# Full array shapes for the products that use 64 rows, 16 rows, 64 columns or 16 columns

## The chip, the cores and the metric

The kernel runs on one core of a Trainium2 chip. The metric is device time in microseconds (us) of one execution; the runs shown are whole executions of the program. A core has five engines with instruction queues of their own: TensorE (PE; its weight loads are listed as PEld), VectorE (DVE), ScalarE (ACT), GpSimd (POOL) and SyncE (SP), which here issues nearly all DMAs.

## The reference

Two transformer blocks run one after the other on 2048 tokens of width 1024, all in float32. The first has eight heads of "forgetting" attention (causal, with a bias from cumulated gates) and eight query heads of sliding-window attention over two key heads, with a sink. The second puts 16 meta tokens in front of the sequence; its attention chooses 256 keys for each query by an index score and always sees the meta tokens, beside a gated linear recurrence (HGRN2):

```python
s = jnp.einsum('bnqhgd,bnshd->bnhgqs', qb, kk, ...) * (d ** -0.5)      # sliding window: 128 queries x 256 keys
...
s_h = jax.nn.relu(jnp.einsum('bqhd,bkd->bqhk', qib, ki_r)... * (IDX_DIM ** -0.5))
s_idx = jnp.einsum('bqhk,bqh->bqk', s_h, wib.astype(jnp.float32))      # index score, 4 heads of 64
s_idx = jnp.where(causal[None], s_idx, -jnp.inf)
_, sel = lax.top_k(s_idx, k_top)                                       # 256 keys of each query
...
p = jax.nn.softmax(jnp.concatenate([lg_m, lg_s], axis=-1), axis=-1)    # meta keys and chosen keys
return (jnp.einsum('bhqm,bmc->bqhc', p[..., :N_META], c_m) + jnp.einsum('bqhk,bqkc->bqhc', p[..., N_META:], c_sel))
...
new_state = (jnp.exp(b_last[:, :, 0, :])[..., None] * state            # HGRN2, chunks of 64
             + jnp.einsum('bhsk,bhsv->bhkv', kc * jnp.exp(b_last - bcum), vc))
```

## The kernel before

Float32 operands are split into a high and a low float16 half, and a product is done as high x high, high x low and low x high into one float32 accumulator. `load_q` and `load_k` put a head's queries and keys into tiles of 128 rows with two planes. Plane 0 (`QA`, `KA`) holds the high half in rows 0 to 63, and a few rows more below it for terms that are added by the product itself: rows 64 and 65 of `KA` hold two powers of two (from `d_kc`), and rows 64 and 65 of `QA` are written later, by `Att.max_rows`, with each query's row maximum cut into these two steps. Plane 1 (`QB`, `KB`) holds the cross terms of high and low in 128 rows.

A head goes through two passes. `prepare` loads it and computes scores in the orientation queries x keys from the high halves alone, to find each query's maximum on VectorE; `max_rows` then turns the maxima into rows 64 and 65 of `QA`. `main` computes the scores again as keys x queries with all terms (`QA` over 66 rows, then `QB`), lets `Att.weights` take the exponential (ScalarE), its float16 high half (ScalarE or VectorE) and the low half (GpSimd or VectorE), and multiplies the weights with the values in `Att.pv` by three products of 65, 64 and 65 columns. `weave` puts the steps of the next head's `prepare` between those of the current head's `main`, so that TensorE's queue mixes both; the steps are placed and ordered by a planner that works from a model of the engines' times. A head is prepared one or two heads ahead, and its tiles come from pools of two buffers, for which the loads wait in SyncE's queue.

The stages in order of time: prologue, projections and forgetting attention of heads 0 to 3 (to some 700 us); heads 4 to 7 with the sliding-window heads woven in, and the output projection (to 1420); index keys, queries and scores of the second block (`Index.scores`, to 1850), with latents between them; the second block's projections (to 2250); the second attention in four query groups g of 512 queries and eight heads each, with the recurrence's chunks and the output projection filled in (`phase_dsa`, to the end).

How the products stand that the change touches:

- The first attention's scores (L959) use 69 rows: 64 and five bias rows.
- The sliding-window scores (L852) and the second attention's scores (L2049) and meta scores (L2061) in `prepare` use rows 0 to 63 of `QA` and `KA`. On L2061 the four query tiles meet 16 meta keys each.
- `Index.scores` sets up queries `QI` in 128 rows (the high half twice) against keys `KI` (high half above low half), and a second product (L1472) of the low queries `QL` in 64 rows against the first 64 rows of `KI`.
- In `phase_dsa.main`, `meta` computes the 16 meta keys x 512 queries (L2083, L2084, and in the first query group L2087 for the bias), so 16 columns of the array are used; the weights of 16 rows then go through `pv` as products over 16 rows (L777 to L779).
- In `Hgrn.chunk` the last of seven scan levels (m = 64) uses 64 columns (L1917 to L1919), the others 128.

Of the kernel before, what the change touches and what calls it, by code (L numbers as in the profile page):

```python
# [10 lines left out]
F32 = mybir.dt.float32  # L11
# [710 lines left out]
class Att:  # L722
# [15 lines left out]

    def weights(self, s, ci):

        K = self.K
        nc = K.nc
        m, n = s.shape
        p = self.pp.tile([128, 512], F32, name="p32")[:m, :n]
        hi = self.pp.tile([128, 512], F16, name="phi")[:m, :n]
        lo = self.pp.tile([128, 512], F16, name="plo")[:m, :n]
        nc.scalar.activation(p, s, AF.Exp, scale=ci[:m], bias=K.shift[:m])  # L747
        if self.pick("hi", n):
            nc.scalar.copy(hi, p)  # L749
        else:  # L750
            nc.vector.tensor_copy(hi, p)
        e = nc.gpsimd if self.pick("lo", n) else nc.vector
        e.tensor_tensor(lo, p, hi, op=ALU.subtract)  # L753
        return hi, lo
# [49 lines left out]
class Swa:  # L804
# [31 lines left out]
    def prepare(self, g, h):  # L836
        K, op, sm = self.K, self.op, self.sm
        nc = K.nc
        if h % 4 == 0:
            self.load(g, h // 4)  # L840
        KA = self.keys[g, h // 4][0]
        Q = op.tile([128, 2, 512], F16, name="sQ")
        load_q(K, Q, K.d_qb, h, g * 512)
        QA, QB = Q[:, 0], Q[:, 1]
        mx = sm.tile([128, 4], F32, name="smx")
        es = sm.tile([128, 4, 1], F32, name="es")

        def score(s):
            k0 = 128 if g == 0 and s == 0 else s * 128
            w = 128 if g == 0 and s == 0 else 256  # L850
            p = self.ps1.tile([128, 512], F32, name="p1")
            nc.tensor.matmul(p[:, :w], lhsT=QA[:64, s * 128:s * 128 + 128], rhs=KA[:64, k0:k0 + w],  # L852
                             start=True, stop=True)
            jk = sm.tile([128, 256], BF, name="jk", bufs=1)
            nc.vector.tensor_tensor_reduce(jk[:, :w], p[:, :w], K.mR2[:, 256 - w:], 1.0, self.sks[:, h:h + 1],
                                           op0=ALU.add, op1=ALU.max, accum_out=mx[:, s:s + 1])

        def rows():
            z = self.at.max_rows(mx, QA)
            nc.vector.scalar_tensor_tensor(es[:, :, 0], z[:, :, 64], STEPS[0] / STEPS[1], z[:, :, 65], op0=ALU.mult,  # L860
                                           op1=ALU.add)
            nc.scalar.activation(es, es, AF.Exp, scale=self.ci[:, h // 4:h // 4 + 1], bias=self.sk[:, h:h + 1])

        return (QA, QB, es), [lambda s=s: score(s) for s in range(4)] + [rows]
# [377 lines left out]
def phase_proj2(K, A, E, finish):  # L1242
    nc, tc = K.nc, K.tc
    K.wbufs, K.rbufs, K.wpool = 6, 4, WPOOL[1]
    with ExitStack() as st:
# [47 lines left out]
        def latent(p, m, col, inv):  # L1293
# [32 lines left out]
            for t in range(tn):  # L1326
# [7 lines left out]
                if tw < 128:  # L1334
                    nc.gpsimd.memset(v2, 0.0)
                nc.gpsimd.memset(v2[:, :, 0:1], 1.0)
                split2(K, v2[:tw, :, 1:65], v2[:tw, :, 65:129], pv.rearrange("p (h d) -> p h d", h=8), 2.0 ** -20)
# [109 lines left out]
class Index:  # L1447
# [11 lines left out]
    def scores(self, i):  # L1459
        K, sc, KI, wi = self.K, self.sc, self.KI, self.wi  # L1460
        nc = K.nc
        QI = sc.tile([128, 4, 128], F16, name="QI")
        QL = sc.tile([64, 4, 128], F16, name="QL")
        for (dst, a) in ((QI[:64], 0), (QI[64:], 0), (QL, 1)):
            nc.sync.dma_start(dst, ap(K.d_qi, a * S + i * 128, [[2 * S, 64], [128 * S, 4], [1, 128]]))
        for u in range(i // 4 + 1):
            w = min(512, (i + 1) * 128 - u * 512)
            acc, ac2 = (sc.tile([128, 512], F32, name=n, bufs=b)[:, :w] for n, b in (("acc", 2), ("ac2", 1)))
            for h in range(4):
                p = self.psc.tile([128, 512], F32, name="psc")  # L1470
                nc.tensor.matmul(p[:, :w], lhsT=QI[:, h], rhs=KI[:, u * 512:u * 512 + w], start=True, stop=False)
                nc.tensor.matmul(p[:, :w], lhsT=QL[:, h], rhs=KI[:64, u * 512:u * 512 + w], start=False, stop=True)  # L1472
                t, f = (acc, ac2)[h % 2], wi[:, i, h:h + 1]
# [337 lines left out]
class Hgrn:  # L1811
# [58 lines left out]
    def chunk(self, t):  # L1870
# [35 lines left out]
        for li, m in enumerate(LEVELS):  # L1906
# [6 lines left out]
            p = self.py.tile([128, 8, 64], F32, name="pl", tag="y")  # L1913
            M = 64 if m == 64 else 128
            for h in range(8):
                qv = [x[:, h].rearrange("p (n a m) -> p n a m", a=2, m=m)[:, :, 1] for x in (hi, lo)]
                nc.tensor.matmul(p[:M, h], lhsT=hi[:, h, :M], rhs=qv[0], start=True, stop=False)  # L1917
                nc.tensor.matmul(p[:M, h], lhsT=hi[:, h, :M], rhs=qv[1], start=False, stop=False)
                nc.tensor.matmul(p[:M, h], lhsT=lo[:, h, :M], rhs=qv[0], start=False, stop=True)  # L1919
            if m == 64:  # L1920
# [58 lines left out]
def phase_dsa(K, A, out):  # L1979

    nc, tc = K.nc, K.tc
    with ExitStack() as st:
# [12 lines left out]

        jr, jb = K.jr, K.jb
        lg = os_.tile([128, D], F32, name="lg")
        lb = wp.tile([128, D], F32, name="lbb")
# [18 lines left out]
        def prepare(g, h, mk):  # L2017
            n = (g + 1) * 512
            x = "0" if g == 0 and h % 2 == 0 else ""
            Q = op.tile([128, 2, 512], F16, name="QA", tag="QA" + x)  # L2020
            load_q(K, Q, K.d_q2, h, g * 512)
            QA, QB = Q[:, 0], Q[:, 1]

# [12 lines left out]
            if g == 0:  # L2036

                bM = op.tile([16, 2, 256], F32R, name="bM")
                bMb = op.tile([16, 128], BF, name="bMb")
                nc.sync.dma_start(f32(bM), ap(K.d_rb, h * 512 + 128, [[1, 16], [8 * 512, 2], [1, 256]]))  # L2040
                nc.sync.dma_start(bMb, ap(K.d_rbb, h * 512 + 128, [[1, 16], [1, 128]]))
            mu = sm.tile([128, 4, 5], F32, name="mu", tag="mu" if g else "mu0")[:, :, :g + 2]

            def score(s, u):
# [3 lines left out]
                near = [(j, 0 if j == i else 128) for j in (i - 1, i) if j >= 0 and j // 4 == u]  # L2048
                nc.tensor.matmul(p[:, :w], lhsT=QA[:64, s * 128:s * 128 + 128], rhs=KA[:64, 16 + u * 512:16 + u * 512 + w],  # L2049
                                 start=True, stop=not near)  # L2050
# [7 lines left out]
            def meta():  # L2058
                p = ps1.tile([128, 512], F32, name="p1")
                for s in range(4):  # L2060
                    nc.tensor.matmul(p[:, s * 16:s * 16 + 16], lhsT=QA[:64, s * 128:s * 128 + 128],  # L2061
                                     rhs=KA[:64, :16], start=s == 0, stop=False, skip_group_check=True)
                if g == 0:
                    nc.tensor.matmul(p[:, :16], lhsT=bMb, rhs=jb[:16, 112:], start=False, stop=True,
                                     skip_group_check=True)
# [11 lines left out]
        def main(g, h, ops, mk):  # L2077
# [3 lines left out]
            def meta():  # L2081
                p = pst.tile([128, 512], F32, name="pst")[:16]
                nc.tensor.matmul(p, lhsT=KA[:66, :16], rhs=QA[:66], start=True, stop=False)  # L2083
                nc.tensor.matmul(p, lhsT=KB[:, :16], rhs=QB, start=False, stop=g > 0)  # L2084
                if g == 0:
                    for a in range(2):
                        nc.tensor.matmul(p[:, :256], lhsT=jr[:16, 112:], rhs=bM[:, a], start=False, stop=a == 1)  # L2087
                hi, lo = at.weights(p, K.dci[:, h // 4:h // 4 + 1])
                for s in range(4):
                    c = slice(s * 128, s * 128 + 128)  # L2090
                    at.pv(po[:, s], hi[:, c], lo[:, c], v[:16, 0], first=s == 0)

# [236 lines left out]
```

## Time and profile before

| | |
|---|---|
| median of 3 runs | 3256.96 us (3254.07 to 3264.24) |
| profiled execution | 3269.84 us, of which the span from first to last instruction is 3267.9 us |
| mean granted clock of TensorE | 0.931 |
| busy: TensorE, VectorE, ScalarE, GpSimd | 2968.1, 2112.4, 1691.4, 1439.1 us |
| moved from and to memory | 243.94 and 112.82 MB |

An instruction's row names its line in the kernel, its engine, what it writes and reads, its shape, a count and a duration. For a matmul, "64*128 64x512" is 64 rows and 128 columns of the array and a moving operand of 64 partitions by 512 elements. Matmuls are pipelined and their recorded ends are modelled; a row's duration is a latency, and the distance between two starts tells how long TensorE is occupied. "Busy" of a stage counts the union of the instructions' times. PEclk is the share of its full clock that TensorE was granted.

### The profile page before, as it was taken

To read this page: it belongs to the slowest core of one execution; us is meant where nothing else is said; L and a number is where in the kernel's file an instruction comes from. 1 tells how busy PE (TensorE), PEld (TensorE's weight loads), DVE (VectorE), ACT (ScalarE), POOL (GpSimd) and SP (SyncE) were. 2 spreads that over 40 slices of the span, in tenths; PEclk is the share of its full clock that TensorE was granted. 3 is DMA by queue.
4 is the path that set the end of the run, shared out by engine and by line. 5 is a ranking of instruction groups with operands and counts; after the bars stand their busy time and mean duration, and the time that the engine had idled before them with its cause. 6 is when DMAs were issued, how large, how long until landed. Compare 5 with 4: busy or idle time off the path is not lost. (4 is left out here: it accounts for less than half of the span.)

```text
span 3267.9 us, 65762 instructions
## 1 busy us (share of the span) xinstructions
PE 2968.1 (91%) x25152; PEld 1853.2 (57%) x25152; DVE 2112.4 (65%) x5073; ACT 1691.4 (52%) x3058; POOL 1439.1 (44%) x1239
## 2 busy tenths in 40 slices
PE   6899999999996899899999899898888899899997
PEld 5554445577873555544445684366666466566554
DVE  7523866566668676646598799611777678778554
ACT  4423755566566555533365575222655456556663
POOL 2311456644234554423233515511556466667552
PEclk9899999999996999999999899898769989989998
DMA  6232344432334443234334531314544533333331
GB/s 236 76 92 75 115 125 127 145 95 66 94 103 145 118 131 118 81 107 139 97 94 107 166 104 64 111 65 127 146 114 119 162 99 92 103 102 102 105 94 57
DMA packets 264430, 361.16 MB, mean 111 GB/s; under 512 B 55372, under 2 KB 185280, under 8 KB 262952
## 3 DMA queue, kind: packets, MB, share of 16 engines
q1 hardware_dynamic: 263672, 356.84, 36.1%
q8 instruction: 199, 3.26, 0.4%
q14 instruction: 127, 1.04, 0.1%
q10 hardware_dynamic: 432, 0.02, 0.0%
HBM read 243.94 MB, written 112.82 MB: 109 GB/s over the span
## 5 line engine op out<-in xcount | busy, mean ns | idle before, releaser
L753 POOL TENSOR_TENSOR plo<-p,phi 128x512 f16<-128x512 f32 (+4 forms) x628 | 693.8, 1116 | 733.5 <-ACT phi L749 458.4
L749 ACT CAST phi<-p 128x512 f16<-128x512 f32 (+4 forms) x681 | 367.5, 557 | 132.8 <-PE po L779 101.0
L747 ACT ACTIVATE p<-pst,shift,dci 128x512 f32<-128x512 f32 (+4 forms) x352 | 247.5, 716 | 152.0 <-PE pst L2110 69.3
L777 PE MATMUL po<-v,phi 128*128 128x65 f16 (+1 forms) x2304 | 303.2, 197 | 10.7 <-ACT phi L749 7.7
L779 PE MATMUL po<-v,plo 128*128 128x65 f16 (+1 forms) x2304 | 285.2, 196 | 27.2 <-POOL plo L753 21.5
L778 PE MATMUL po<-v,phi 128*128 128x64 f16 (+1 forms) x2304 | 302.0, 198 | 0.0
L779 PEld LDWEIGHTS <-plo 128*128 128x128 f16 (+1 forms) x2552 | 245.3, 101 | 76.0 <-POOL plo L753 38.0
L777 PEld LDWEIGHTS <-phi 128*128 128x128 f16 (+1 forms) x2552 | 246.6, 99 | 57.8 <-ACT phi L749 14.1
L747 ACT ACTIVATE p<-pst,shift,fci 128x512 f32<-128x512 f32 (+1 forms) x320 | 218.9, 710 | 110.1 <-PE pst L984 61.3
L963 DVE TENSOR_REDUCE mu<-p 128x1 f32<-128x512 f32 (+2 forms) x320 | 188.1, 603 | 128.6 <-PE p L959 86.4
L2055 DVE CUSTOM_DVE_ANT_0 jk<-p,mk 128x512 bf16<-128x512 f32 (+2 forms) x320 | 193.5, 605 | 105.7 <-PE p L2049 49.3
L284 POOL TENSOR_TENSOR wlo<-wraw,whi 128x512 f16<-128x512 f32 (+3 forms) x116 | 151.0, 1319 | 240.8 <-ACT whi L283 214.0
L778 PEld LDWEIGHTS <-phi 128*128 128x128 f16 (+1 forms) x2552 | 246.7, 100 | 13.8 <-issue 2.6
L337 PE MATMUL pp<-whi,hhi 128*128 128x256 f16 (+2 forms) x824 | 235.0, 286 | 8.0 <-ACT whi L283 5.7
L339 PE MATMUL pp<-whi,hlo 128*128 128x256 f16 (+2 forms) x824 | 233.0, 285 | 5.0 <-POOL hlo L465 5.0
L338 PE MATMUL pp<-wlo,hhi 128*128 128x256 f16 (+2 forms) x824 | 234.8, 285 | 0.6 <-POOL wlo L284 0.6
L326 PE MATMUL pp<-hhi,whi 128*128 128x512 f16 (+2 forms) x496 | 190.1, 383 | 2.7 <-DVE ra L523 2.7
L328 PE MATMUL pp<-hhi,wlo 128*128 128x512 f16 (+2 forms) x496 | 190.0, 383 | 0.0
L327 PE MATMUL pp<-hlo,whi 128*128 128x512 f16 (+2 forms) x496 | 189.8, 383 | 0.0
L328 PEld LDWEIGHTS <-wlo 128*128 128x128 f16 (+2 forms) x1000 | 100.1, 101 | 123.8 <-issue 13.4
L326 PEld LDWEIGHTS <-whi 128*128 128x128 f16 (+2 forms) x1000 | 100.6, 101 | 120.4 <-issue 14.7
L327 PEld LDWEIGHTS <-whi 128*128 128x128 f16 (+2 forms) x1000 | 100.1, 101 | 113.7 <-issue 16.1
(655 smaller groups left out, 8815.5 us busy)
## 6 DMA issues: line engine op xcount, KB each, us to landing
wraw<-in_w_in_dram SPq DMA_DIRECT2D x88, 256.0 KB
d_z<-er SPq DMA_DIRECT2D x128, 128.0 KB
bT<-d_rb SPq DMA_DIRECT2D x32, 384.0 KB
wa<-in_w_ada_dram SPq DMA_DIRECT2D x8, 1024.0 KB
x<-in_x_dram SPq DMA_DIRECT2D x16, 512.0 KB
d_k<-ehi SPq DMA_DIRECT2D x32, 256.0 KB
d_q<-ehi SPq DMA_DIRECT2D x32, 256.0 KB
QA<-d_q SPq DMA_DIRECT2D x64, 128.0 KB
```

The lines of the kernel that those rows point to most:

```text
L326: nc.tensor.matmul(ps, lhsT=whi, rhs=hhi[:, kk, :], start=kk == 0, stop=False)
L327: nc.tensor.matmul(ps, lhsT=whi, rhs=hlo[:, kk, :], start=False, stop=False)
L328: nc.tensor.matmul(ps, lhsT=wlo, rhs=hhi[:, kk, :], start=False, stop=kk == KK - 1)
L337: nc.tensor.matmul(ps, lhsT=hhi[:, kk, s], rhs=whi, start=kk == 0, stop=False)
L338: nc.tensor.matmul(ps, lhsT=hhi[:, kk, s], rhs=wlo, start=False, stop=False)
L339: nc.tensor.matmul(ps, lhsT=hlo[:, kk, s], rhs=whi, start=False, stop=kk == KK - 1)
L747: nc.scalar.activation(p, s, AF.Exp, scale=ci[:m], bias=K.shift[:m])
L749: nc.scalar.copy(hi, p)
L753: e.tensor_tensor(lo, p, hi, op=ALU.subtract)
L777: nc.tensor.matmul(o, lhsT=hi, rhs=v[:, :65], start=first, stop=False, **kw)
L778: nc.tensor.matmul(o[:, 1:65], lhsT=hi, rhs=v[:, 65:129], start=False, stop=False, **kw)
L779: nc.tensor.matmul(o, lhsT=lo, rhs=v[:, :65], start=False, stop=last, **kw)
```

## The change

Products that use at most 64 rows or columns of the array are widened, with operands that add nothing:

- `prepare` of the sliding-window and of the second attention loads two rows of zeros (from `d_qx`) into rows 64 and 65 of `QA`, and the score products run over 66 rows; zeros meet the two constants in `KA`. `max_rows` later overwrites these rows, as before. That is one small DMA more for each of 64 heads and query groups.
- `QL` is loaded twice, into both halves of 128 rows, so that the low queries meet the high and the low half of the index keys: one DMA more for each of 14 query tiles, and a low x low term that was left out before.
- The meta keys' scores are computed for 128 columns (the 16 meta keys and the first 112 keys behind them), of which 16 are used. Their weights go into two fixed tiles `wm` of 128 rows, filled with zeros once on GpSimd, whose first 16 rows are rewritten for each head; `pv` runs over all 128 rows. For that the ones in the first value column are set only in the 16 meta rows. The bias rows `bM` and `bMb` are loaded for 128 partitions in place of 16, from an offset lower by 112, and meet the whole of the reversal matrices `jr` and `jb`.
- The last scan level uses 128 columns like the others.

The diff, cut to its core:

```diff
-    def weights(self, s, ci):
+    def weights(self, s, ci, dst=None):
...
-        hi = self.pp.tile([128, 512], F16, name="phi")[:m, :n]
-        lo = self.pp.tile([128, 512], F16, name="plo")[:m, :n]
+        hi, lo = (x[:m, :n] for x in dst or [self.pp.tile([128, 512], F16, name=x) for x in ("phi", "plo")])
...
         load_q(K, Q, K.d_qb, h, g * 512)
+        nc.sync.dma_start(Q[64:66, 0], K.d_qx[0, :2])
...
-            nc.tensor.matmul(p[:, :w], lhsT=QA[:64, s * 128:s * 128 + 128], rhs=KA[:64, k0:k0 + w],
+            nc.tensor.matmul(p[:, :w], lhsT=QA[:66, s * 128:s * 128 + 128], rhs=KA[:66, k0:k0 + w],
...
-                nc.gpsimd.memset(v2[:, :, 0:1], 1.0)
+                nc.gpsimd.memset(v2[:tw, :, 0:1], 1.0)
...
-        QL = sc.tile([64, 4, 128], F16, name="QL")
-        for (dst, a) in ((QI[:64], 0), (QI[64:], 0), (QL, 1)):
+        QL = sc.tile([128, 4, 128], F16, name="QL")
+        for (dst, a) in ((QI[:64], 0), (QI[64:], 0), (QL[:64], 1), (QL[64:], 1)):
...
-                nc.tensor.matmul(p[:, :w], lhsT=QL[:, h], rhs=KI[:64, u * 512:u * 512 + w], start=False, stop=True)
+                nc.tensor.matmul(p[:, :w], lhsT=QL[:, h], rhs=KI[:, u * 512:u * 512 + w], start=False, stop=True)
...
-            M = 64 if m == 64 else 128
...
-                nc.tensor.matmul(p[:M, h], lhsT=hi[:, h, :M], rhs=qv[0], start=True, stop=False)
+                nc.tensor.matmul(p[:, h], lhsT=hi[:, h], rhs=qv[0], start=True, stop=False)
...
+        wm = [wp.tile([128, 512], F16, name=f"wm{x}") for x in ("hi", "lo")]
+        for x in wm:
+            nc.gpsimd.memset(x, 0.0)
...
             load_q(K, Q, K.d_q2, h, g * 512)
+            nc.sync.dma_start(Q[64:66, 0], K.d_qx[0, :2])
...
-                bM = op.tile([16, 2, 256], F32R, name="bM")
-                bMb = op.tile([16, 128], BF, name="bMb")
+                bM = op.tile([128, 2, 256], F32R, name="bM")
+                bMb = op.tile([128, 128], BF, name="bMb")
...
-                nc.tensor.matmul(p[:, :w], lhsT=QA[:64, s * 128:s * 128 + 128], rhs=KA[:64, 16 + u * 512:16 + u * 512 + w],
+                nc.tensor.matmul(p[:, :w], lhsT=QA[:66, s * 128:s * 128 + 128], rhs=KA[:66, 16 + u * 512:16 + u * 512 + w],
...
-                p = pst.tile([128, 512], F32, name="pst")[:16]
-                nc.tensor.matmul(p, lhsT=KA[:66, :16], rhs=QA[:66], start=True, stop=False)
-                nc.tensor.matmul(p, lhsT=KB[:, :16], rhs=QB, start=False, stop=g > 0)
+                p = pst.tile([128, 512], F32, name="pst")
+                nc.tensor.matmul(p, lhsT=KA[:66, :128], rhs=QA[:66], start=True, stop=False)
+                nc.tensor.matmul(p, lhsT=KB[:, :128], rhs=QB, start=False, stop=g > 0)
...
-                hi, lo = at.weights(p, K.dci[:, h // 4:h // 4 + 1])
+                hi, lo = wm
+                at.weights(p[:16], K.dci[:, h // 4:h // 4 + 1], (hi, lo))
...
-                    at.pv(po[:, s], hi[:, c], lo[:, c], v[:16, 0], first=s == 0)
+                    at.pv(po[:, s], hi[:, c], lo[:, c], v[:, 0], first=s == 0)
```

More of the change, by code (lines that the diff above doesn't have):

```diff
@@ L1913, in chunk @@
             p = self.py.tile([128, 8, 64], F32, name="pl", tag="y")
-            M = 64 if m == 64 else 128
             for h in range(8):
                 qv = [x[:, h].rearrange("p (n a m) -> p n a m", a=2, m=m)[:, :, 1] for x in (hi, lo)]
-                nc.tensor.matmul(p[:M, h], lhsT=hi[:, h, :M], rhs=qv[0], start=True, stop=False)
-                nc.tensor.matmul(p[:M, h], lhsT=hi[:, h, :M], rhs=qv[1], start=False, stop=False)
-                nc.tensor.matmul(p[:M, h], lhsT=lo[:, h, :M], rhs=qv[0], start=False, stop=True)
+                nc.tensor.matmul(p[:, h], lhsT=hi[:, h], rhs=qv[0], start=True, stop=False)
+                nc.tensor.matmul(p[:, h], lhsT=hi[:, h], rhs=qv[1], start=False, stop=False)
+                nc.tensor.matmul(p[:, h], lhsT=lo[:, h], rhs=qv[0], start=False, stop=True)
             if m == 64:
@@ L2036, in prepare @@
             if g == 0:
-                bM = op.tile([16, 2, 256], F32R, name="bM")
-                bMb = op.tile([16, 128], BF, name="bMb")
-                nc.sync.dma_start(f32(bM), ap(K.d_rb, h * 512 + 128, [[1, 16], [8 * 512, 2], [1, 256]]))
-                nc.sync.dma_start(bMb, ap(K.d_rbb, h * 512 + 128, [[1, 16], [1, 128]]))
+                bM = op.tile([128, 2, 256], F32R, name="bM")
+                bMb = op.tile([128, 128], BF, name="bMb")
+                nc.sync.dma_start(f32(bM), ap(K.d_rb, h * 512 + 16, [[1, 128], [8 * 512, 2], [1, 256]]))
+                nc.sync.dma_start(bMb, ap(K.d_rbb, h * 512 + 16, [[1, 128], [1, 128]]))
             mu = sm.tile([128, 4, 5], F32, name="mu", tag="mu" if g else "mu0")[:, :, :g + 2]
@@ L2060, in meta @@
                 for s in range(4):
-                    nc.tensor.matmul(p[:, s * 16:s * 16 + 16], lhsT=QA[:64, s * 128:s * 128 + 128],
-                                     rhs=KA[:64, :16], start=s == 0, stop=False, skip_group_check=True)
+                    nc.tensor.matmul(p[:, s * 16:s * 16 + 16], lhsT=QA[:66, s * 128:s * 128 + 128],
+                                     rhs=KA[:66, :16], start=s == 0, stop=False, skip_group_check=True)
                 if g == 0:
-                    nc.tensor.matmul(p[:, :16], lhsT=bMb, rhs=jb[:16, 112:], start=False, stop=True,
+                    nc.tensor.matmul(p[:, :16], lhsT=bMb, rhs=jb[:, :16], start=False, stop=True,
                                      skip_group_check=True)
@@ L2081, in meta @@
             def meta():
-                p = pst.tile([128, 512], F32, name="pst")[:16]
-                nc.tensor.matmul(p, lhsT=KA[:66, :16], rhs=QA[:66], start=True, stop=False)
-                nc.tensor.matmul(p, lhsT=KB[:, :16], rhs=QB, start=False, stop=g > 0)
+                p = pst.tile([128, 512], F32, name="pst")
+                nc.tensor.matmul(p, lhsT=KA[:66, :128], rhs=QA[:66], start=True, stop=False)
+                nc.tensor.matmul(p, lhsT=KB[:, :128], rhs=QB, start=False, stop=g > 0)
                 if g == 0:
                     for a in range(2):
-                        nc.tensor.matmul(p[:, :256], lhsT=jr[:16, 112:], rhs=bM[:, a], start=False, stop=a == 1)
-                hi, lo = at.weights(p, K.dci[:, h // 4:h // 4 + 1])
+                        nc.tensor.matmul(p[:, :256], lhsT=jr, rhs=bM[:, a], start=False, stop=a == 1)
+                hi, lo = wm
+                at.weights(p[:16], K.dci[:, h // 4:h // 4 + 1], (hi, lo))
                 for s in range(4):
                     c = slice(s * 128, s * 128 + 128)
-                    at.pv(po[:, s], hi[:, c], lo[:, c], v[:16, 0], first=s == 0)
+                    at.pv(po[:, s], hi[:, c], lo[:, c], v[:, 0], first=s == 0)
             def block(j):
```

## The prediction

> **What bounds the kernel now.** I read the page's busy shares first, then the stages, then TensorE's own instructions in order of time, then the waits.
>
> ```profile
> span 3267.9 us, 65762 instructions
> PE 2968.1 (91%) x25152; PEld 1853.2 (57%) x25152; DVE 2112.4 (65%) x5073; ACT 1691.4 (52%) x3058; POOL 1439.1 (44%) x1239
> ```
>
> ```profile
> core 0: us, PE busy (x) PEld busy (x) DVE busy (x) ACT busy (x) POOL busy (x), PEclk, DMA share, GB/s
> 700.00:1420.00 720.00, 650.08 (x6410) 436.70 (x6409) 472.91 (x1268) 414.69 (x765) 307.57 (x269) 0.93 0.34 105
> 1420.00:1850.00 430.00, 413.05 (x2271) 210.49 (x2270) 310.34 (x726) 200.49 (x426) 146.03 (x151) 0.96 0.40 117
> 2250.00:2430.00 180.00, 149.56 (x1424) 103.94 (x1422) 117.39 (x274) 93.49 (x161) 83.99 (x69) 0.70 0.57 151
> 2430.00:3215.00 785.00, 722.01 (x7905) 471.76 (x7901) 552.20 (x1148) 454.63 (x742) 481.79 (x378) 0.94 0.36 104
> ```
>
> The second fence is the windows view of the four stages that the change touches (sliding-window heads, index scores, first and later query groups of the second attention). In all four TensorE (PE) is the busiest: 90%, 96%, 83% and 92% of the stage; the next, VectorE, has 66%, 72%, 65% and 70%. A matmul's recorded time is a latency, so I look at the distance from one start to the next. Here is the timeline of TensorE in the first attention, whose scores have 69 rows, and then in the second:
>
> ```profile
> 305.65 0.38 PE L959 MATMUL p<-KA,QA 69*128 69x512 f16 x1
> 305.87 0.22 PE L962 MATMUL p<-mR,idb 128*128 128x128 bf16 x1
> ```
>
> ```profile
> 2830.18 0.38 PE L2098 MATMUL pst<-QA,KA 66*128 66x512 f16 x1
> 2830.49 0.39 PE L2049 MATMUL p<-KA,QA 64*128 64x512 f16 x1
> 2830.81 0.23 PE L2052 MATMUL p<-jb,bTb 128*128 128x128 bf16 x1
> ...
> 2833.09 0.19 PE L1919 MATMUL pl<-Xh,Xl 128*128 128x64 f16 x1
> 2833.21 0.20 PE L777 MATMUL po<-v,phi 16*128 16x65 f16 x1
> 2833.25 0.19 PE L778 MATMUL po<-v,phi 16*128 16x64 f16 x1
> 2833.37 0.23 PE L2049 MATMUL p<-KA,QA 64*128 64x128 f16 x1
> ...
> 2834.01 0.39 PE L2098 MATMUL pst<-QA,KA 66*128 66x512 f16 x1
> 2834.24 0.38 PE L2099 MATMUL pst<-QA,KA 128*128 128x512 f16 x1
> ```
>
> The first number of "66*128" is the rows of the array that a product uses, the second its columns. A product over 512 elements is followed after 0.22 or 0.23 us when both it and its successor use over 64 rows: 305.65 to 305.87 behind 69 rows, 2834.01 to 2834.24 behind 66. But from 66 rows to 64 rows it takes 0.31 us (2830.18 to 2830.49) and from 64 back to 128 it takes 0.32 (2830.49 to 2830.81). A product over 64 or 65 elements is followed after 0.04 (2833.21), but after 0.12 where the next uses 16 rows in place of 128, or 64 in place of 16 (2833.09, 2833.25). So each change between array shapes costs 0.08 to 0.10 us on TensorE, in which no other engine is waited for: an excursion there and back costs up to 0.20.
>
> **The change part by part.** *Products that get the full shape.* These are all that leave it in the four stages (L1918 and L1919 share L1917's count, L2084 that of L2083, L778 and L779 that of L777):
>
> ```profile
> L852 PE MATMUL p<-sK,sQ x128: 226/279/393, 755.3 to 1374.5; 64*128 64x256 f16 x120, 64*128 64x128 f16 x8
> L1472 PE MATMUL psc<-KI,QL x152: 226/386/606, 1425.5 to 1829.4; 64*128 64x512 f16 x112, 64*128 64x384 f16 x16, 64*128 64x128 f16 x12, 64*128 64x256 f16 x12
> L2049 PE MATMUL p<-KA,QA x320: 212/386/606, 2257.3 to 3179.0; 64*128 64x512 f16 x128, 64*128 64x128 f16 x16, 64*128 64x384 f16 x16
> L2061 PE MATMUL p<-KA,QA x128: 166/166/192, 2255.3 to 3151.1; 64*128 64x16 f16 x128
> L2083 PE MATMUL pst<-QA,KA x32: 376/383/596, 2273.1 to 3187.7; 66*16 66x512 f16 x32
> L777 PE MATMUL po<-v,phi 16*128 16x65 f16 x128 | 18.4, 196 | 1.7 <-ACT phi L749 1.6
> L1917 PE MATMUL pl<-Xh 128*64 128x64 f16 x64 | 9.4, 216 | 2.3 <-ACT Xh L1911 2.3
> ```
>
> The first three rows are single products among full ones: 128 + 152 + 320 = 600 excursions. The meta work comes in groups, three per head and query group (L2061 in fours, L2083 with L2084, L777 to L779 in twelves): 32 x 3 = 96. The last scan level is 8 groups. That is 704 excursions x 0.20 = 141 us as a ceiling. Followed product by product through the timeline, 1399 of these 1408 switches stand there; behind 1326 the pause is short enough (under 0.15 us) that nothing else was waited for, and those pauses add up to 127 us: 23, 29, 13 and 62 in the four stages.
>
> What of it lies on the path? Where TensorE is bound, all; where it waits for others, a switch saved turns into a longer wait. I let 0.7 pass in the first stage, 0.85 in the second and the fourth (busy 96% and 92%), 0.5 in the third, where TensorE idles 30 of 180 us and the clock is low: 16 + 25 + 6 + 53 = 100 us. What is late next is shown by TensorE's present waits in these stages:
>
> ```profile
> PE po L779 <- POOL plo L753: 21.5, 33, 2.3
> PE p L2049 <- DVE mu L2055: 15.4, 13, 2.9
> PE p L2061 <- DMA KA<-d_k: 6.8, 8, 1.6
> PE p L959 <- DMA KA<-d_kx: 5.8, 5, 2.6
> ```
>
> They are the reason for 0.85 and not 1: GpSimd's low halves and VectorE's maxima get no faster. All of the 127 and none of it are the two ends.
>
> The products themselves cost the same with more rows or columns (0.22 and 0.23 us behind 69 and 66 rows; 64 rows at 512 elements take 0.32 with the pause). The bias load of the meta keys, L2087, now brings in 128 columns of 32-bit weights; L2108 does that today in 190 ns against 97, sixteen times: 1.5 us.
>
> ```profile
> L2087 PEld LDWEIGHTS pst<-bM,jr x16: 87/97/109, 2274.1 to 2378.1; 16*16 16x16 f32 x16
> L2108 PEld LDWEIGHTS pst<-bT,jr x240: 186/190/338, 2275.0 to 3210.0; 128*128 128x128 f32 x120
> ```
>
> *Added loads.* 64 loads of two zero rows (2 KB) behind the two query loads, one per head, and 14 second copies of the low index queries.
>
> ```profile
> L943 SPq DMA_DIRECT2D QA<-d_qx x32: 273/477/508, 120.6 to 1301.5; - x32
> L1465 SPq DMA_DIRECT2D QL<-d_qi x14: 573/574/614, 1420.3 to 1758.1; - x14
> bM<-d_rb SPq DMA_DIRECT2D x8, 32.0 KB
> bMb<-d_rbb SPq DMA_DIRECT2D x8, 4.0 KB
> SPq L379 <- PE pst L2099: 85.7, 19, 16.4
> ```
>
> SyncE's queue spends 0.48 us on such a load (L943, the same load in the first attention) and 0.57 on an index load: 64 x 0.48 + 14 x 0.57 = 39 us of queue time over 2000 us. Behind them queue the key, value and bias loads of the same head, and stores. The head is loaded one or two heads ahead, so I cost it at nothing but for heads whose keys are late already: the 8 waits at L2061, 0.5 us more each, 4 us. With the cover gone it is 39 us. The bias rows of the first query group grow from 36 to 288 KB on 8 heads, 2 MB; the stage's 151 GB/s at a share of 0.57 make 265 GB/s at full share, so 1 us a head. Two heads at the stage's start are uncovered: 2 us (all eight: 8).
>
> *Fixed tiles for the meta weights.* Two fills on GpSimd, before the second attention. No row shows a fill of that size: 0.13 us each by the small fill (L1336, 128x8) to 1.2 by the 128x512 subtraction:
>
> ```profile
> L1336 POOL MEMSET vt<- 128x8 f16 x17 | 2.2, 133 | 41.0 <-DMA d_vf<-vt 35.4 <-DVE B L1705 3.8 <-DVE X L1724 1.7
> L753 POOL TENSOR_TENSOR plo<-p,phi 128x512 f16<-128x512 f32 x421 | 518.8, 1242 | 457.0 <-ACT phi L749 279.2 <-PE po L779 36.5 <-PE pst L984 25.6
> ```
>
> GpSimd waits 457 us there in all, so nothing, or 2.4 us uncovered. One pair in place of a rotating one makes a head's meta weights wait for the previous head's meta products, a whole head earlier: nothing. The narrower fill of the value column saves nothing that can be seen.
>
> Sum: -100 + 1.5 + 4 + 2 = -92 us. The profiled execution took 3269.8 us (span 3267.9); 3178 remain. The median of the runs is 0.996 of that execution, so 3165 us.
>
> **A rule weighed against the rows.** The pause at a switch is 0.08 to 0.10 us in the rows above. The Trainium skill says of it, in "TensorEngine Tiling (Array Packing)", section Key Properties, that a change of tiling mode drains TensorE, and in "TensorE: Matmul & The Clock Gate", section Step-by-step, that a drain is some 128 cycles; at the 2.4 GHz of that page this gives an estimate of 53 ns a switch and 74 us in place of 127 before the shares above. The rows have nearly twice that, and the sum goes by them.
>
> **The rivals.** *The pause is the weight load.* A 64-row load can't be laid under the running product, and with 66 rows it stays so. Then nothing goes: 3257 + 7 = 3264 us. For it: pauses sit just at the products with their own weights. Against it: L959 and L2098 load weights of 69 and 66 rows for each product and show no pause. The Trainium skill ("TensorE: Matmul & The Clock Gate", section The mechanism) states that weight loads overlap a running product only where the row groups differ (another section adds a background buffer); by the first, the full-row products should pause too; the trace does not agree, with 0.22 us from start to start at 512 elements.
>
> *Another engine takes over.* GpSimd and VectorE already make TensorE wait (rows above). If only 0.4 of the 127 passes: 3257 - 51 + 7 = 3213.
>
> *The clock comes back.* With the granted clock at 0.93, 0.96, 0.70 and 0.94, the four stages spend 2 x (0.07 x 720 + 0.04 x 430 + 0.30 x 180 + 0.06 x 785) = 337 us at half clock (the granted clock is taken as either full or half). A stream without pauses may win it back sooner. If a fifth of these 337 us ran at full clock, with TensorE busy, 34 us would go besides: 3131. Against it: a faster TensorE also idles more.
>
> *Slower: the third load is late.* The first score of each of 64 heads now needs one more load at the end of a queue that already waits for free buffers (L379, up to 16.4 us). If that is seen by TensorE, it costs at most about 2.6 us a head (the longest wait at L959, whose tile has the same third load): 64 x 2.6 = 166 us against 92 gained, 3257 + 74 = 3331. It decides from 36 exposed heads on. Against it: L959 waited only 5 times in all for its rows.
>
> **How the numbers follow.** Forecast with its shares as taken 0.67, other engine 0.13, clock 0.11, weight load 0.05, late load 0.04. The forecast's own span runs from all of 127 us passing (3257 - 127 + 7 = 3137) to the loads' cover gone (3165 + 39 = 3204). The order of instructions is planned anew from a changed program, which no row prices; I add 10 us at both sides, as the three runs shown differ by that. With the takeover at 3213 and half of the clock's cases the range is 3110 to 3225. Under 0.3% (10 us) a measurement of this kernel can't be told from no change. Faster by more than that: 0.91; within it 0.05 (the weight load); slower 0.04.
>
> **What would show it.** After the change, L2049, L852 and L1472 stand with 66, 66 and 128 rows and are followed after 0.22 us at 512 elements; the fourth stage loses some 53 us, the second 25, and the stages before 700 us and from 1850 to 2250 none. TensorE's waits for GpSimd's low halves at L779 grow. The prediction is wrong if the pauses stay, if the waits at L779 and L2049 grow by more than 60 us together, or if the zero-row load is what L2049, L2061 or L852 wait for. The doubled low queries change the index scores a little; if the quick threshold search then missed a row, the repeat branch would run the second attention again, 965 us by the last two of the four stages. Nothing in the trace points to that, and I give it no chance of its own.

## The result and the profile after

The changed kernel takes 3170.52 us, median of 6 runs (3164.58 to 3174.09), against 3261.30 us for the kernel before in 6 runs (3254.07 to 3272.39): a ratio of 0.9709, 95% interval 0.9686 to 0.9732, some 95 us less (91 between the medians). The forecast was 3165 us. Its first two lines of the page, to be held against the first two of before:

```profile
span 3168.7 us, 65862 instructions
PE 2822.7 (89%) x25152; PEld 1858.8 (59%) x25152; DVE 2101.6 (66%) x5073; ACT 1686.9 (53%) x3058; POOL 1450.2 (46%) x1241
```

TensorE runs the same 25152 products and is busy for 145.4 us less (2968.1 to 2822.7), but the span is only 99.2 us shorter. So some 46 us of what TensorE gave back became idle time of TensorE. The windows view shows in which stage. For this comparison the windows of both kernels are cut at the ends of the same work: sliding-window heads, index scores, the second block's projections (which the change does not touch), second attention. Before:

```profile
core 0: us, PE busy (x) PEld busy (x) DVE busy (x) ACT busy (x) POOL busy (x), PEclk, DMA share, GB/s
700.00:1425.00 725.00, 655.08 (x6433) 438.95 (x6432) 474.39 (x1270) 415.37 (x766) 307.57 (x269) 0.93 0.34 105
1425.00:1829.00 404.00, 387.32 (x2063) 190.28 (x2062) 296.38 (x697) 188.98 (x397) 137.64 (x143) 0.95 0.39 113
1829.00:2274.00 445.00, 398.99 (x2698) 267.44 (x2696) 258.63 (x723) 183.51 (x328) 135.92 (x87) 0.93 0.31 101
2274.00:3268.00 994.00, 890.19 (x9367) 580.62 (x9366) 690.52 (x1430) 548.75 (x904) 572.74 (x453) 0.89 0.38 109
```

After:

```profile
core 0: us, PE busy (x) PEld busy (x) DVE busy (x) ACT busy (x) POOL busy (x), PEclk, DMA share, GB/s
700.00:1397.00 697.00, 640.22 (x6465) 449.81 (x6463) 465.33 (x1273) 418.56 (x768) 311.72 (x270) 0.92 0.36 110
1397.00:1788.00 391.00, 356.57 (x2036) 195.76 (x2034) 290.02 (x685) 180.84 (x382) 137.53 (x141) 0.96 0.41 115
1788.00:2238.00 450.00, 398.70 (x2728) 271.08 (x2728) 264.56 (x736) 189.81 (x344) 137.31 (x92) 0.94 0.33 105
2238.00:3169.00 931.00, 792.47 (x9365) 568.50 (x9364) 691.59 (x1430) 543.80 (x904) 579.57 (x453) 0.92 0.41 118
```

The second number of a row is the stage's length, the third TensorE's busy time; the first less the second is its idle time. The stages change by -28, -13, +5 and -63 us. In the index stage TensorE's busy time falls by 30.8 us, and its idle time doubles from 16.7 to 34.4. In the second attention it falls by 97.7 us, and idle time grows from 103.8 to 138.5.

The forecast put no saving into the projections; they take 5 us longer, with the same busy time of TensorE (399.0 and 398.7 us).

That the pauses are gone is seen in the timeline of TensorE after the change, at three places: second attention, index scores, sliding-window heads. The first number is the start:

```profile
2408.10 0.38 PE L2087 MATMUL pst<-QA,KA 66*128 66x512 f16 x1
2408.32 0.38 PE L2088 MATMUL pst<-QA,KA 128*128 128x512 f16 x1
2408.54 0.38 PE L2052 MATMUL p<-KA,QA 66*128 66x512 f16 x1
2408.76 0.22 PE L2055 MATMUL p<-jb,bTb 128*128 128x128 bf16 x1
...
1641.44 0.38 PE L1471 MATMUL psc<-KI,QI 128*128 128x512 f16 x1
1641.66 0.38 PE L1472 MATMUL psc<-KI,QL 128*128 128x512 f16 x1
1641.87 0.38 PE L327 MATMUL pp<-x1lo,whi 128*128 128x512 f16 x1
...
900.92 0.20 PE L777 MATMUL spo<-sv,phi 128*128 128x64 f16 x1
900.95 0.27 PE L852 MATMUL p<-sK,sQ 66*128 66x256 f16 x1
901.06 0.27 PE L337 MATMUL pp<-whi,hhi 128*128 128x256 f16 x1
```

L2052 (L2049 before) and L1472 start 0.22 us behind their predecessors and are followed after 0.22 and 0.21 us at 512 elements; L852 is entered after 0.03 and followed after 0.11 at 256. Counted product by product through the whole trace, 1533 changes between shapes with some 151 us of pauses became 138 with 12 us; 8 of these 12 us lie before 700 us, which the change does not touch. The Trainium skill ("TensorEngine Tiling (Array Packing)", section Key Properties) states that changing the tiling mode drains TensorE; the trace agrees as to what pauses, and has 94 to 103 ns for a change at full clock.

What is late next is in TensorE's waits over the whole execution (us in all, times, longest):

```profile
PE p L768 <- DVE zrow L765: 36.2, 15, 8.4
PE po L778 <- POOL plo L752: 27.9, 38, 3.3
PE p L2052 <- DVE mu L2058: 21.1, 20, 3.7
PE psc L1471 <- DVE acc L1475: 10.0, 8, 2.1
PE psc L1471 <- ACT rl L1478: 6.7, 8, 2.2
PE p L2067 <- DMA bMb<-d_rbb: 5.0, 1, 5.0
PE p L2064 <- DMA KA<-d_kc: 3.7, 3, 1.7
```

GpSimd's low halves went from 21.5 to 27.9 us (L778 was L779), VectorE's maxima in front of L2052 from 15.4 to 21.1. The index scores' waits and that at L768 stood like this before:

```profile
PE p L769 <- DVE zrow L766: 33.1, 16, 6.2
PE psc L1471 <- ACT rl L1478: 3.5, 3, 1.5
PE psc L1471 <- DVE acc L1475: 2.8, 4, 1.2
```

Many waits grow by a few us each, and none takes over.

### The profile page after: what moved, and what is told of

The parts are those of the page before. It is cut to its first block, busy times and chain, and to the rows that moved or that the text cites. A ratio compares the mean times of both kernels' runs of the same rounds, so it can differ in the third digit from the quotient of the medians.

```text
span 3168.7 us, 65862 instructions
## 1 busy us (share of the span) xinstructions
PE 2822.7 (89%) x25152; PEld 1858.8 (59%) x25152; DVE 2101.6 (66%) x5073; ACT 1686.9 (53%) x3058; POOL 1450.2 (46%) x1241
## 5 line engine op out<-in xcount | busy, mean ns | idle before, releaser
L752 POOL TENSOR_TENSOR plo<-p,phi 128x512 f16<-128x512 f32 (+3 forms) x600 | 664.9, 1121 | 569.9 <-ACT phi L748 360.0
L748 ACT CAST phi<-p 128x512 f16<-128x512 f32 (+3 forms) x649 | 347.0, 554 | 84.2 <-PE po L778 75.1
L778 PE MATMUL po<-v,plo 128*128 128x65 f16 x2176 | 270.1, 196 | 35.0 <-POOL plo L752 27.9
L776 PE MATMUL po<-v,phi 128*128 128x65 f16 x2176 | 286.4, 197 | 5.3 <-ACT phi L748 4.2
L777 PE MATMUL po<-v,phi 128*128 128x64 f16 x2176 | 285.3, 198 | 0.0
L778 PEld LDWEIGHTS <-plo 128*128 128x128 f16 x2424 | 234.7, 101 | 79.2 <-POOL plo L752 46.8
L776 PEld LDWEIGHTS <-phi 128*128 128x128 f16 x2424 | 236.1, 100 | 48.8 <-ACT phi L748 11.4
L777 PEld LDWEIGHTS <-phi 128*128 128x128 f16 x2424 | 235.6, 100 | 15.3 <-issue 1.8
```

What stands on the lines that cost most here:

```text
L776: nc.tensor.matmul(o, lhsT=hi, rhs=v[:, :65], start=first, stop=False, **kw)
L777: nc.tensor.matmul(o[:, 1:65], lhsT=hi, rhs=v[:, 65:129], start=False, stop=False, **kw)
L778: nc.tensor.matmul(o, lhsT=lo, rhs=v[:, :65], start=False, stop=last, **kw)
```

## The experiments

The theory: the pause belongs to the change of shape on TensorE, part of it passes to the time, and the rest turns into waits for the other engines. The first rival: it belongs to a weight load that cannot be laid under a running product. The second: loads are what decides. Ratios are to the kernel before, run beside each kernel on the same chip.

**The parts one by one.** Four kernels take the kernel before and one part of the change each.

*Only the second attention's scores and meta scores on 66 rows, with their zero loads:*

```diff
             load_q(K, Q, K.d_q2, h, g * 512)
+            nc.sync.dma_start(Q[64:66, 0], K.d_qx[0, :2])
-   lhsT=QA[:64, ...], rhs=KA[:64, ...]      # L2049, L2061
+   lhsT=QA[:66, ...], rhs=KA[:66, ...]
```

> Of the change only the second attention's score and meta-score products (L2049, L2061) on 66 rows, with their zero-row loads. Theory (the pause at a change of array shape is the gain): 320 + 32 excursions x 0.20 us = 70 us less on TensorE, of which some two thirds pass: 3215 us, 46 less than before. Rival (the gain comes from a new order by the planner or from the meta tiles): within 10 us of before, or a gain out of step with the count of excursions.

Measured 3229.42 us, ratio 0.9905 (0.9882 to 0.9928), some 31 us less where 46 were expected.

*Only the doubled low index queries:*

```diff
-        QL = sc.tile([64, 4, 128], F16, name="QL")
-        for (dst, a) in ((QI[:64], 0), (QI[64:], 0), (QL, 1)):
+        QL = sc.tile([128, 4, 128], F16, name="QL")
+        for (dst, a) in ((QI[:64], 0), (QI[64:], 0), (QL[:64], 1), (QL[64:], 1)):
-                nc.tensor.matmul(..., lhsT=QL[:, h], rhs=KI[:64, ...])
+                nc.tensor.matmul(..., lhsT=QL[:, h], rhs=KI[:, ...])
```

> Of the change only the doubled low index queries (L1472). Theory: 152 excursions, 30 us less on TensorE; the trace of the whole change has the index stage 13 us shorter and the projections behind it 4 us longer, so VectorE and ScalarE take most of it: 3250 us, 11 less. As I predicted it, with 0.85 passing: 3236. Rival (order): no relation to the count.

Measured 3256.10 us, ratio 0.9984 (0.9967 to 1.0002): 5 us less, not told from nothing. The prediction gave this part 25 us. The index stage of its profile, to be held against the second row of before, shows why so little came of it:

```profile
1419.00:1812.00 393.00, 359.16 (x2038) 196.76 (x2037) 290.38 (x685) 181.66 (x383) 138.54 (x141) 0.95 0.40 114
```

TensorE's busy time falls by 28 us and the stage gets 11 us shorter (404 to 393); the other 17 us are idle time.

*Only the sliding-window scores on 66 rows:*

```diff
         load_q(K, Q, K.d_qb, h, g * 512)
+        nc.sync.dma_start(Q[64:66, 0], K.d_qx[0, :2])
-   lhsT=QA[:64, ...], rhs=KA[:64, ...]      # L852
+   lhsT=QA[:66, ...], rhs=KA[:66, ...]
```

> Of the change only the sliding-window scores on 66 rows with their zero-row loads. Theory: 128 excursions, 26 us less on TensorE; the trace of the whole change has this stage 28 us shorter: 3236 to 3245 us. Rival (order): no relation to the count.

Measured 3228.40 us, ratio 0.9898 (0.9879 to 0.9917): 33 us less, more than the 26 that its 128 excursions could give at 0.20 us each. Something besides the pauses moved.

*Only the meta tiles, the wide bias rows and the last scan level* (the change less the three edits above):

> Of the change only the meta tiles of 128 rows and columns with the wider bias rows, and the last scan level on 128 columns; scores and index as before. Theory: 64 meta groups and 8 scan levels, 72 excursions, 14 us less on TensorE less 3 us of wider loads: 3253 us. Rival (the fixed tiles free the rotating weight buffers and that is a main part of the gain): 3230 or less. The four parts together should give the whole's 91 us within 15.

Measured 3251.13 us, ratio 0.9966 (0.9945 to 0.9987): 11 us less for 72 excursions. The product of the four ratios is 0.9755, 80 us less, against 0.9709 for the whole.

**The same source but for the widths.** Every part above also changes the program from which the order of instructions is planned. The next kernel is the changed one with all its loads, tiles and fills, and only the matrix products back on 64 rows. Its loads, tiles and counts of instructions are those of the changed kernel; the planner, however, sees the widths too, and orders part of the program otherwise:

```diff
-   lhsT=QA[:66, ...], rhs=KA[:66, ...]      # L852, L2052, L2064
+   lhsT=QA[:64, ...], rhs=KA[:64, ...]
-   lhsT=QL[:, h], rhs=KI[:, ...]            # L1472
+   lhsT=QL[:64, h], rhs=KI[:64, ...]
```

> The changed kernel with all its loads, fixed meta tiles and wide scan level, but the scores (L2052, L2064, L852) back on 64 rows and the low index product back on 64 rows. Theory (the change of shape alone): 632 excursions are back; the meta part alone gave 3251 and the extra loads cost some 7: 3250 to 3262 us. Rival (a better order by the planner, or anything else in the loads and tiles, made the gain): 3170 to 3200.

Measured 3224.28 us, ratio 0.9891 (0.9857 to 0.9925), where neither theory had it. Its windows, cut at the ends of the same work:

```profile
700.00:1419.00 719.00, 665.91 (x6430) 444.48 (x6428) 466.71 (x1270) 414.09 (x765) 305.79 (x269) 0.92 0.34 106
1419.00:1824.00 405.00, 382.65 (x2032) 186.52 (x2031) 292.52 (x686) 183.06 (x384) 138.37 (x142) 0.96 0.39 111
1824.00:2274.00 450.00, 399.54 (x2727) 269.85 (x2726) 263.42 (x735) 188.77 (x341) 134.25 (x91) 0.93 0.33 105
2274.00:3224.00 950.00, 844.37 (x9367) 565.09 (x9365) 679.45 (x1430) 545.74 (x904) 574.39 (x453) 0.93 0.41 116
```

From here to the changed kernel lie 632 excursions, and a change of order. TensorE's busy time falls by 25.7, 26.1, 0.8 and 51.9 us, 104.5 together; the stages get shorter by 22, 14, 0 and 19 us: 0.86 of the busy time saved in the sliding-window heads, 0.54 in the index scores, 0.37 in the second attention, 0.53 in all; by the medians 3224.28 - 3170.52 = 54 us, 0.51. (One profile each; a few us of each stage are spread.) Held against each other in order of time, the two kernels' products stand in the same order up to TensorE's 7460th, at 952 and 945 us. The index stage has nearly the same order and the projections the same; the rest of the sliding-window heads and most of the second attention are ordered anew. So the shares of these two stages hold the effect of the order too.

What the widths alone do is seen where the order is the same. Here are the kernel before, the kernel with narrow widths and the changed kernel over the same stretch of 2862 products, with 56 of the excursions of L852, cut at the starts of the same two products:

```profile
700.03:953.12 253.09, 249.81 (x2865) 200.56 (x2862) 162.84 (x508) 152.33 (x287) 90.59 (x91) 1.00 0.26 80
699.40:951.69 252.29, 249.81 (x2865) 200.55 (x2862) 162.57 (x508) 152.28 (x287) 90.62 (x91) 1.00 0.26 80
703.48:945.17 241.69, 238.38 (x2865) 202.68 (x2863) 162.14 (x508) 151.67 (x287) 90.86 (x91) 1.00 0.27 84
```

From the second row to the third TensorE's busy time falls by 11.4 us and the time by 10.6, at an unchanged clock: 0.93 passes. Eleven of the fourteen kernels told of here have the same order in this stretch; the six with 64 rows in L852 take 252.3 to 253.6 us for it, the five with 66 rows 241.2 to 244.1. In the index stage, followed product by product, the two longest stretches of common order (1679 products) lose 253 changes of shape with 27.7 us of pauses and get 9.9 us shorter, so 0.36 passes. For the second attention no long stretch of common order exists.

This kernel has the same product shapes as the one with the meta tiles alone, differs from it in 78 more loads and in its planned order, and is 27 us faster by the medians (24 by the ratios). More loads made the kernel slower wherever they were tried (below), so the new order is the likely cause. The difference lies in the second attention, which in the kernel with the meta tiles alone is:

```profile
2275.00:3256.00 981.00, 862.63 (x9367) 574.43 (x9365) 695.76 (x1430) 549.03 (x904) 569.45 (x453) 0.91 0.39 112
```

It has 981 us against 950: 18.3 us more busy time of TensorE at a clock of 0.91 in place of 0.93, and 12.7 us more idle time. That the order does it, and what in it, was not isolated.

**The pause itself.** If it is the weight load of a 64-row product, two such products in a row pause between them too; if it is the change of shape, they do not. L2049 is cut into two halves, 288 products of 64 rows more, on the kernel before:

```diff
-   nc.tensor.matmul(p[:, :w], lhsT=QA[:64, ...], rhs=KA[:64, 16 + u*512 : 16 + u*512 + w], start=True, ...)
+   w0 = w // 256 * 128
+   for a, b in ((0, w0), (w0, w)) if w0 else ((0, w),):
+       nc.tensor.matmul(p[:, a:b], lhsT=QA[:64, ...], rhs=KA[:64, 16 + u*512 + a : 16 + u*512 + b], start=a == 0, ...)
```

> The kernel before, with each second-attention score product of 256 or more columns cut in two along the moving side: 288 more products of 64 rows with weight loads of their own, and no more changes of shape. Theory (the pause belongs to the change of shape): 288 x 0.01 to 0.03 us, at most 9 us slower than before. Rival (each 64-row product pays for its own weight load): 288 x 0.10 = 29 us more on TensorE, 20 to 29 slower, and a distance of 0.21 us between the two halves in place of 0.11 to 0.12.

Measured 3271.76 us, ratio 1.0028 (1.0010 to 1.0047): 9 us more. Its timeline of TensorE, with the cut product (line 2051 there):

```profile
2838.01 0.19 PE L778 MATMUL po<-v,phi 128*128 128x64 f16 x1
2838.14 0.39 PE L2051 MATMUL p<-KA,QA 64*128 64x256 f16 x2
2838.46 0.20 PE L779 MATMUL po<-v,plo 128*128 128x65 f16 x1
```

The row holds both halves. From L778 to the first half it takes 0.13 us where a product over 64 elements alone takes 0.03, and the two halves with the pause behind them take 0.32 us: 2 x 0.11 for 256 elements each, and 0.10. Between the halves there is no pause; their distance has a median of 0.119 us over the trace (0.112 in the next kernel, with 66 rows), where the rival wanted 0.21. The same cut in the changed kernel:

> The same cut in the changed kernel, whose score products use 66 rows: the price of 288 more products without any 64-row load. Theory: 0 to 6 us slower than the changed kernel (3170), and the same step as the cut makes in the kernel before, within 8 us. Rival (weight load): a step at least 20 us smaller than in the kernel before.

Measured 3181.62 us, ratio 0.9758 (0.9726 to 0.9791): 11 us more than the changed kernel by the medians, 16 by the ratios, so no cheaper than before, as the weight-load rival would have had it (and some us above the theory). The cut costs the same with 64 and 66 rows; the weight load is not the pause. The Trainium skill ("TensorE: Matmul & The Clock Gate", section The mechanism) states in one line that weight loads overlap running products only where row groups differ, and a paragraph above that a load into the background weight buffer is pulled ahead as well; here the halves use the same rows, load weights each, and follow each other without a pause, so the one line alone does not hold for this kernel.

**The added loads.** On the changed kernel each zero load is issued a second time, to the same rows:

```diff
+            nc.sync.dma_start(Q[64:66, 0], K.d_qx[0, :2])      # at both places, behind the first
```

> The changed kernel with each zero-row load issued twice: 64 more loads of 2 KB. Theory (they are covered, a head is loaded ahead): 0 to 5 us slower than 3170. Rival (the queue's time of 0.48 us a load or the late landing is seen by TensorE): 31 us slower or more.

Measured 3216.37 us, ratio 0.9855 (0.9818 to 0.9893): 46 us more than the changed kernel, which neither theory had. SyncE's waits in this kernel show what is new (us in all, times, longest):

```profile
SPq L844 <- DMA sQ<-d_qx: 36.3, 27, 3.0
SPq L2026 <- DMA QA<-d_qx: 10.3, 10, 1.9
```

The second load writes where the first does, so it waits in SyncE's queue until the first has landed, and everything behind it in the queue waits too. Neither row exists in the changed kernel's SyncE waits. The waits do not account for the stages, though: the sliding-window heads take some 22 us more than in the changed kernel, with 36.3 us of these waits, and the second attention some 28 us more, with 10.3. So the second load was aimed at rows 66 and 67, which nothing reads:

```diff
+            nc.sync.dma_start(Q[66:68, 0], K.d_qx[0, :2])      # at both places
```

> The changed kernel with a second load of 2 KB of zeros per head into rows 66 and 67 of the query tile, which nobody reads; it need not wait for the first load. Theory (the 46 us of the doubled load came from the second load's wait for the first one's landing, in SyncE's queue, 36 us in 27 waits on the sliding-window's loads alone): 0 to 10 us slower than 3170. Rival (the plain issue of 0.48 us a load costs about 0.7 us of time): 40 to 50 slower.

Measured 3176.37 us, ratio 0.9731 (0.9705 to 0.9757): 6 us more by the medians, 7 by the ratios. So 64 more loads cost about 0.1 us each at most (the two kernels' intervals overlap), and the 40 us beyond that come with the second write to the same rows. That all 40 are the waits in the queue is not shown, since the planner orders the two kernels differently from some 930 us on. Storing the zero rows behind each head's queries in memory, so that one load of 66 rows brings both, was to save even that:

```diff
-            load_q(K, Q, K.d_q2, h, g * 512)
-            nc.sync.dma_start(Q[64:66, 0], K.d_qx[0, :2])
+            load_q66(K, Q, K.d_q2, h, g * 512)      # rows 0 to 65 in one DMA; d_qb, d_q2 as [8, 132, S]
```

> The changed kernel without the 64 zero-row loads: the two zero rows lie behind each head's queries in memory and come with the first query load, so each head has two query loads, as before the change. Theory (the loads are covered): 0 to 8 us faster than 3170. Rival (the loads cost 0.7 us each): 30 us faster or more.

Measured 3268.87 us, ratio 1.0027 (1.0005 to 1.0049): the whole gain lost, against both theories. Among TensorE's waits in this kernel are

```profile
PE p L2070 <- DMA KA<-d_kc: 39.4, 12, 5.7
PE psc L326 <- ACT whi L283: 15.2, 1, 15.2
```

where the changed kernel has 3.7 us for the first (its L2064). The loss is spread: some 17 us in the sliding-window heads, 37 in the projections, which have none of these loads, and 38 in the second attention. Whether the loads of 66 rows land later, the stores into the new layout cost more, or the planner's order got worse, the runs do not separate; this stays open.

**What is next.** GpSimd's share of the low halves is lowered, so that VectorE makes more of them:

```diff
-        at = Att(K, pp, sm, ps1, 1.0, 0.9)
+        at = Att(K, pp, sm, ps1, 1.0, 0.75)
```

> The changed kernel with 0.75 in place of 0.90 of the second attention's low halves on GpSimd, the rest on VectorE. If GpSimd's low halves are what takes over from the pauses: 5 to 15 us faster than 3170. If VectorE's maxima are: 5 to 15 slower. If neither alone: within 5.

Measured 3170.78 us, ratio 0.9719 (0.9683 to 0.9755): no change. TensorE's waits for GpSimd's low halves gave way to waits for VectorE's (24.5 us after 27.9, and 16.7 after 4.8), so neither engine alone holds the second attention.

Last, the same idea on products that the change left: the rotated keys' two halves of 64 columns as one product of 128 columns, 96 products over 512 elements and some 48 changes of shape fewer:

```diff
-                    mm3_T(K, p[a], w, a * m, h[g])      # twice, 64 columns each
+                    mm3_T(K, p, w, 0, h[g])             # once, 128 columns
+                    p = [p[:m], p[m:]]
```

> The changed kernel with the last frequent 64-column products, the rotated keys of the sliding window, as one product of 128 columns for both halves: 96 products of 512 elements less (20.7 us at 0.216) and 50 changes of shape less (5 us). Theory (TensorE bounds that stage too): 15 to 22 us faster than 3170. Rival (others bound it, since VectorE now reads its operands from other partitions and ScalarE and GpSimd follow it): within 5.

Measured 3173.64 us, ratio 0.9724 (0.9693 to 0.9755): no gain, the theory fell. The first 700 us of the changed kernel and of this one:

```profile
0.00:700.00 700.00, 634.71 (x4565) 373.68 (x4566) 390.10 (x950) 353.86 (x663) 284.04 (x287) 0.97 0.38 122
```

```profile
0.00:700.00 700.00, 615.57 (x4451) 364.61 (x4452) 395.74 (x946) 349.97 (x654) 281.86 (x283) 0.94 0.39 122
```

TensorE is busy for 19 us less in the same 700 us, but the work behind it comes no earlier: the index scores begin at 1397.5 us in the changed kernel and at 1406.3 here. The clock there is 0.94 in place of 0.97, and the span ends at 3174.8 us against 3168.7. In the newly planned order the saving became idle time. No kernel here beats the changed one.

## Why the prediction was right, and where its terms were off

**The mechanism was right.** The pause goes with the change of shape: it is missing between two 64-row products, and missing behind 66 rows. The weight-load rival (3264 us) fell by the timeline of the changed kernel and by both cuts. Where order and clock are the same, 11.4 us less busy time are 10.6 us less time.

**The stages.** Predicted were savings of 53 us in the second attention's later groups and 6 in its first, 25 in the index scores, 16 in the sliding-window heads and none elsewhere; measured were 63 in the second attention, 13, 28, and a loss of 5 in the projections. Only the second attention and "none elsewhere" came near.

**The step that failed: the share that passes.** The prediction took 0.85 for the index scores and the later groups, from TensorE's busy share of 96% and 92%, and 0.7 for the sliding-window heads at 90%. In the index scores 0.54 of the busy time saved passes by the kernel that differs in the widths, 0.42 by the whole change (13 of 31 us), 0.39 by the low index queries alone (11 of 28), and 0.36 of the pauses where the order is the same: 13 us in place of 25. A busy share of 96% hid that the next engines were close; the waits of L1471 for VectorE and ScalarE grew from 6.3 to 16.7 us. In the sliding-window heads 0.93 passes where the order is the same (TensorE is busy for 99% of that stretch, which the 90% of the whole stage hid), and the stage gained 28 us in place of 16. So the share was too high in the busier of the two stages and too low in the other. For the second attention the runs give no clean share: 0.37 by the kernel with narrow widths and 0.55 by the scores on 66 rows alone (994 to 959 us, with 63 us less busy time), both with a new order.

**What made the total good.** The index scores fell short by 12 us, the projections lost 5, the sliding-window heads gave 12 more than forecast and the second attention 4 more (before the forecast's costs of 7.5): errors in opposite directions, which cancelled. That the second attention came out at 63 us is partly luck too. The kernel with the meta tiles alone and the one with narrow widths have the same product shapes, and take 981 and 950 us there. The order, for which the prediction allowed 10 us to either side, is the likely cause of these 31 us, and how much of the 63 it gave the runs do not tell. Of 100 us before the costs, the prediction's own division gives 632 of the 704 excursions about 90 (all but the 72 of 424 in the second attention, 10 of its 59 us); from the kernel with narrow widths to the changed one they brought 54, and the other 36 were there without them, of which the prediction had 10 - 7.5 = 2.5.

**The clock.** The second attention was granted 0.89 of the full clock before and 0.92 after, and 0.93 with the widths back at 64 rows. Its two parts, before and then after:

```profile
2274.00:2454.00 180.00, 157.51 (x1599) 111.29 (x1599) 129.44 (x280) 105.39 (x182) 97.72 (x82) 0.74 0.51 137
2454.00:3268.00 814.00, 732.68 (x7770) 469.33 (x7769) 561.07 (x1150) 443.36 (x722) 475.02 (x372) 0.93 0.35 103
```

```profile
2238.00:2418.00 180.00, 136.82 (x1627) 111.63 (x1626) 135.00 (x288) 105.92 (x184) 99.68 (x82) 0.79 0.58 155
2418.00:3169.00 751.00, 655.65 (x7741) 456.87 (x7738) 556.59 (x1143) 437.89 (x721) 479.89 (x372) 0.95 0.37 110
```

So the rival "the clock comes back" was in part there in this profile: counted through the trace, the products' excess at half clock fell by some 20 us over the whole execution. It did not come on top of the forecast as the rival had it. Since the kernel with narrow widths has as high a clock, and the one with another share for GpSimd, as fast as the changed kernel, has only 0.91 in that stage, it is not tied to the missing pauses (one profile each). What grants it was not tried.

**The costs.** The loads were rightly covered: 64 more of them cost 6 us, against 39 us with the cover gone. "The third load is late" (3331 us) did not come: the zero rows appear in no wait of TensorE, and L2064 waited 4 times for its keys where L2061 had waited 8. The 4 us for late keys were not seen. The bias rows cost one wait of 5.0 us at the first head (L2067), where the same product (L2064 in the kernel before) had waited 1.6 us: 3.4 more, predicted 2 for two heads. The waits at L778 and L2052 grew by 6.4 and 5.7 us, the direction predicted and far below the 60 that would have refuted it.

## What to carry to other kernels

A lone product on 64 rows (or fewer rows or columns) among full ones costs two pauses of about 0.1 us, whatever its length; two rows of zeros remove them, and with loads one or two heads ahead these cost next to nothing, as long as no load writes what an earlier one still writes. What part of such a saving passes is not read from a stage's busy share: look at how close the next engines stand there, and allow for a third (index scores) as well as for nearly all (the stretch of the sliding-window heads). Where a planner orders the instructions anew, every edit carries an uncertainty of its own (some 25 us of 3261 between two kernels here). Even a kernel that differs in one width alone is planned anew; only a stretch in which both kernels keep the same order tells the edit from the order.

## What the runs showed of the hardware that was not expected

- A change of shape costs 94 to 97 ns into and 102 to 103 ns out of a 64-row product at full clock, and 112 to 138 ns at half. 16 rows, 16 columns and 64 columns cost about the same (88 to 96 ns); 66 and 69 rows cost nothing to either side of products with 128.
- Two products in a row with weights of their own on the same 64 rows follow each other without a pause (0.119 us for 256 elements).
- A small load that waits for an earlier one to the same place blocks SyncE's queue for 1.0 to 1.3 us on average (36.3 us in 27 waits, 10.3 in 10). A kernel with 64 such loads takes 46 us more, with the same loads to other rows 6, each in an order of its own.
